# Output projection: two reloads of input rows moved ahead of the loads of a stored operand

## The chip, the cores and the metric

The kernel runs on one core of a Trainium2 chip. A core has a matrix engine (TensorE, PE in the profile), three engines for elementwise work (VectorE or DVE, ScalarE or ACT, GpSimd or POOL), SyncE (SP), which here only issues DMA transfers, and 16 DMA engines that move data between DRAM and the on-chip memory. Each engine works through its own instructions in a fixed order and waits on semaphores for the others. The metric is the time on the device in microseconds (us); the median of several runs is compared.

## The reference

One layer of a hybrid encoder, in float32, on 1024 tokens with 1024 channels. The part that matters here is the output projection and what follows it:

```python
merged = g_a * (o_sb @ w_o_sb) + g_b * (o_hg @ w_o_hg)
h = x + merged @ w_out
hn = rmsnorm(h, norm2_g)
a = square(relu(hn @ w_ff1))
h = h + a @ w_ff2
```

All matrices of `h = x + merged @ w_out` are 1024 x 1024.

## The kernel before

**Arithmetic.** Each float32 operand is split into a high part (a cast on ACT, line 144) and a low part (a subtraction on DVE, line 149). A product is three matmuls per tile: high by high, high by low, low by high (`three`, line 510). The helper `sub` or `add` shows in the profile as line 1118 or 1115, every matmul as line 121, and every load on SP's queue as line 129.

**The output projection** (`out_start`, line 1559) is computed by a scheme of seven half-size products: `merged` and `w_out` are cut in four quarters, sums of quarters are formed beforehand, and each product has 512 x 512 x 512 elements. It is done in four row blocks of 128 tokens (`tb` 0 to 3); a product of one block is 12 matmuls (`out_product`, line 1541). The blocks run through these passes:

1. `oW` (pwW in the profile): product "11" by "11", into one PSUM bank for each block. ACT copies the bank twice to `hres[tb]`, and DVE subtracts it from `hres[4 + tb]`, which holds the x rows of this block (line 1577).
2. `oW` again: "12" by "21" is added into the same bank. PE may start a block of it only after DVE's subtraction of pass 1 has read the bank.
3. `oX` (pwX): "2" by "2" into a new bank, followed by a subtraction on DVE.
4. `oX` again: "3" by "3" on top, with a subtraction, then "a" by "4".
5. `oY` (pwY): "1" by "1", then "4" by "22" (`out_block_done`, line 1623). Each finished block is squared and summed on ACT, its inverse root is taken on POOL, and DVE normalises it (`norm2_token`, line 1485). PE then transposes the normalised rows (`hnt`).

**Where the operands come from.** The x rows are reloaded from DRAM into the tiles `h4` to `h7` (`hres[4]` to `hres[7]`, in the order of the row blocks 1 to 4). The operands "2", "3", "a", "1" and "4" of `merged` (`m2r`, `m3r` and so on) are sums of quarters that the stage before formed. POOL stored them to DRAM (`fd`, `put`, line 1438), and SP loads them back (`out_operands`, line 1518). The last of these stores is issued at the end of the gate stage, so the second load of each operand has to wait for it. The weights "2", "3", "4", "1" (`wout2r` and so on) come from DRAM as well (`tw`).

**What sets the order.** `load` (line 128) chains every load on SP behind the load before it, so SP issues them in the order of the program text. A load that waits for a store holds all loads behind it. `in_turn` (line 135) fixes the order on ACT and DVE in the same manner. For row block 2, `out_operands(m=["2"], behind=True)` (line 1581) issues the two loads of "2" at once and leaves its splits for after the loop. In the loop of pass 1 the loads stand so on SP: h4, two of wout21, two of wout2, h5, two of m2, h6, h7, then two of wout3 and two of m3. POOL adds x rows to `hres[0]` to `hres[3]` with accumulating transfers (line 1596), which run at the same time.

Of the kernel before, what the change touches and what calls it, by code (L numbers as in the profile page):

```python
# [22 lines left out]
NT = T // P  # L23
# [16 lines left out]
def kernel(  # L40
# [20 lines left out]
    X = x[0]  # L61
# [13 lines left out]
    def slot(name, dt=F32):  # L75
        return spool.tile([P, 1024], dt, tag="s", name=name)
# [7 lines left out]
    def bank(name):  # L84
        return psum.tile([P, 512], F32, tag="p", name=name)
# [12 lines left out]
    def after(ins, earlier):  # L98
        if earlier is not None and earlier.ins is not ins.ins:
            tc.add_manual_dep(ins.ins, earlier.ins.name, NOSYNC, reason="issue order")  # L100
        return ins
# [26 lines left out]
    def load(dst, src):  # L128
        last_load[0] = after(nc.sync.dma_start(dst, src), last_load[0])
# [5 lines left out]
    def in_turn(engine, ins):  # L135
        if turns["on"]:
            after(ins, turns[engine])
            turns[engine] = ins
        return ins
# [12 lines left out]
    def hi_lo(h, l, src):  # L152
        hi_copy(h, src)
        return lo_sub(l, src, h)
# [300 lines left out]
    class Stream:  # L455
# [6 lines left out]
        def add(self, units, body):  # L462
            self.jobs.append((units, body))
            return len(self.jobs)
# [652 lines left out]
    def sub(out, a, b):  # L1117
        return nc.vector.tensor_tensor(out=out, in0=a, in1=b, op=ALU.subtract)
# [15 lines left out]
    def out_block(i, j):  # L1134
        return W_OUT[i * 512 : (i + 1) * 512, j * 512 : (j + 1) * 512]
# [342 lines left out]
    hres = []  # L1478
# [32 lines left out]
    def out_unit(name, src):  # L1511
        pieces = [src[i * 256 : (i + 1) * 256, :].rearrange("(k p) c -> p k c", p=P) for i in range(2)]
        return Unit(f"wout{name}", [[(0, 512, t)] for t in pieces], wide=True)
# [4 lines left out]
    def out_operands(w=(), m=(), behind=False):  # L1518

        for n in w:  # L1520
            out_form[n] = out_unit(n, tw[int(n)] if len(n) == 1 else out_block(int(n[0]) - 1, int(n[1]) - 1))
            out_form[n].split()
        for n in m:
            merged[n] = []
            raw = []
            for kp in range(2):
                r = slot(f"m{n}r{kp}")
                load(r.rearrange("p (k t) -> p k t", k=2), fd[n][kp])
                h, l = slot(f"m{n}h{kp}", F32R), slot(f"m{n}l{kp}", F32R)
                merged[n].append((h, l))  # L1530
                raw.append(r)

            def split(n=n, raw=raw):
                for (h, l), r in zip(merged[n], raw):
                    hi_lo(h, l, r)

            if behind:
                return split
            split()

    def out_product(ps, a, w, tb, start):
        open_block("fill")
        for k in range(4):
            c = k % 2 * 512
            sh, sl = (t[:, c + tb * P : c + (tb + 1) * P] for t in merged[a][k // 2])
            wh, wl = (t[:, c : c + 512] for t in out_form[w].hl[k // 2])
            three(ps, sh, sl, wh, wl, start and k == 0, k == 3, True)


    def rows(tb):  # L1550
        return slice((tb + 4) % NT * P, ((tb + 4) % NT + 1) * P)
# [4 lines left out]
    def turn_dve(ins):  # L1556
        in_turn("dve", ins)

    def out_start():

        merged["11"] = [mgs.t[0, kp] for kp in range(2)]
        merged["12"] = [mgs.t[0, kp] for kp in range(2, 4)]
        for tb in range(NT):
            hres.append(slot(f"h{tb}"))
        for tb in range(4):
            load(hres[4 + tb], X[rows(4 + tb), :])
            if tb == 0:
                out_operands(["21"])
            oW[tb] = bank(f"pwW{tb}")
            out_product(oW[tb], "11", "11", tb, True)  # L1570
            for ins in (
                nc.scalar.activation(hres[tb][:, right], oW[tb], AF.Identity, scale=-1.0),
                nc.scalar.copy(hres[tb][:, left], oW[tb]),
            ):
                in_turn("act", ins)
            h = hres[4 + tb][:, right]
            turn_dve(sub(h, h, oW[tb]))
            if tb == 0:
                out_operands(["2"])
            if tb == 1:  # L1580
                m2 = out_operands(m=["2"], behind=True)
        m2()
        for tb in range(4):
            out_product(oW[tb], "12", "21", tb, False)
            h = hres[4 + tb][:, left]
            turn_dve(add(h, h, oW[tb]))
            if tb == 0:
                out_operands(["3"])
            if tb == 1:
                out_operands(m=["3"])  # L1590
        for tb in range(4):
            oX[tb] = bank(f"pwX{tb}")
            out_product(oX[tb], "2", "2", tb, True)
            h = hres[4 + tb][:, right]
            turn_dve(sub(h, h, oX[tb]))
            nc.gpsimd.dma_start(hres[tb], X[rows(tb), :], accum_op=ALU.add)
            if tb == 0:
                out_operands(["4"])
            if tb == 1:
                out_operands(m=["a"])  # L1600
        for tb in range(4):
            out_product(oX[tb], "3", "3", tb, False)
            h = hres[tb][:, right]
            turn_dve(sub(h, h, oX[tb]))
            if tb == 0:
                out_operands(["1"])
            if tb == 1:
                out_operands(m=["1"])
            if tb > 1:
                pairs[tb - 2].load()  # L1610

        for tb in range(4):
            u = pairs[tb % 2]
            (u.split if tb < 2 else u.sums)()
            out_product(oX[tb], "a", "4", tb, False)
            h = hres[tb][:, left]
            turn_dve(add(h, h, oX[tb]))
            if tb == 2:
                out_operands(["22"])
            if tb == 3:  # L1620
                out_operands(m=["4"])
# [489 lines left out]
    first = pairs[:2]  # L2111
    turns["on"], turns["act"], turns["dve"] = True, None, None
    out_start()
    g2b[0] = slot("g2b")
    load(g2b[0], norm2_g[0].partition_broadcast(P))
# [91 lines left out]
```

## Time and profile before

The page gives the span of the profiled execution and no other time of it; the runs were timed apart.

| | |
|---|---|
| time, median of 3 runs | 1453.28 us (1452.68 to 1454.21) |
| span of the profiled execution | 1450.7 us |
| busy: PE, DVE, ACT, POOL | 1436.6, 1098.2, 669.8, 142.0 us |
| output projection, passes 1 to 4, on PE | from 742.9 to 803.9 us |
| DMA, mean over the span | 156 GB/s |

The span runs from the first to the last instruction of the program. Start times in the timeline are microseconds from its beginning; a row gives start, duration, engine, line, operation, tiles (written <- read), the form, the number of instructions merged in the row, and in brackets the engine's idle time before it with what ended it. "SPq" is SP issuing a transfer: the duration is that of the issue and not of the transfer, and where two issues are merged in one row, of all from the first to the last. The chain of waits follows the work that ended last from its end back to what released it. Rows of the windows view give, for a stretch of time, its length, the busy time of PE, of PE's weight loads, DVE, ACT and POOL, and at the end the granted clock of PE (1.00 is full), the busy share of the 16 DMA engines and their GB/s.

### The profile page before, as it was taken

The page shows a single profiled execution, that of the slowest core. Times are in us where ns is not written, and L with a number is a line of the kernel's source. Part 1 is how long each engine was busy: PE and PEld are TensorE (multiplying, and loading weights), DVE is VectorE, ACT ScalarE, POOL GpSimd, SP SyncE. Part 2 cuts the span into 40 slices and gives each one's busy share as a digit, 9 for nine tenths or more (in the row PEclk, how much of TensorE's full clock was granted, in tenths as well). Part 3 has the DMA queues.
Part 4 walks back from the last instruction along what each step waited for, and adds up shares of the span by engine and source line. Part 5 has one row for each costly group of instructions (what it writes and reads, how often), then busy time and mean ns, then how long its engine had stood idle before and what let it go on. Part 6 is the DMA issues. An engine that isn't in the chain of part 4 may idle for free.

```text
span 1450.7 us, 19961 instructions
## 1 busy us (share of the span) xinstructions
PE 1436.6 (99%) x7464; PEld 1222.6 (84%) x7464; DVE 1098.2 (76%) x1561; ACT 669.8 (46%) x1156; POOL 142.0 (10%) x340
## 2 busy tenths in 40 slices
PE   9999999999999999999999999999999999999998
PEld 8989988988898888888877888888888888888886
DVE  6699899798747797887757898666666757768765
ACT  7566666652323243533334575444444533523443
POOL 3121121110000012100010200000000000000032
PEclk9999999999999999999999999999999999999999
DMA  7234154321303349655479414344445974676825
GB/s 211 48 98 103 37 95 81 59 44 52 102 16 102 73 137 261 225 170 182 144 217 306 166 59 153 138 159 153 152 160 189 341 273 183 249 273 245 282 100 185
DMA packets 157881, 225.73 MB, mean 156 GB/s; under 512 B 25644, under 2 KB 93784, under 8 KB 157784
## 3 DMA queue, kind: packets, MB, share of 16 engines
q1 hardware_dynamic: 142520, 183.29, 37.3%
q0 software_dynamic: 11520, 34.61, 9.5%
q10 hardware_dynamic: 3744, 6.56, 1.2%
q8 instruction: 59, 0.97, 0.3%
q14 instruction: 38, 0.31, 0.1%
HBM read 162.55 MB, written 61.87 MB: 155 GB/s over the span
## 4 chain that ended last, share of the span: by engine, by line
PE 95%; DVE 1%; ACT 1%; DMA 1%; issue 1%; POOL 1%; POOLq 0%; DVEq 0%; ACTq 0%
PE pm L121 21%; PE pX L121 9%; PE pW L121 6%; PE pY L121 6%; PE pjqk L121 6%; PE pji L121 3%; PE pga L121 3%; PE pjq L121 3%; PE pys L121 3%; PE gY L121 3%; PE gX L121 3%; PE pyh L121 3%; PE pjf L121 3%; PE pjg L121 3%; PE sl L121 2%; PE po L121 2%
## 5 line engine op out<-in xcount | busy, mean ns | idle before, releaser
L144 ACT CAST whid<-w 128x1024 fp32r<-128x1024 f32 x30 | 31.6, 1053 | 153.0 <-PE pm L121 85.1
L709 DVE TENSOR_TENSOR_SCAN rm<-rm,bits 128x511 f32<-128x511 f32 (+7 forms) x72 | 87.3, 1220 | 14.3 <-ACT rm L687 12.8
L121 PE MATMUL pm<-wlod,sh 128*128 128x512 f32 x240 | 93.5, 390 | 0.0
L121 PE MATMUL pm<-whid,sl 128*128 128x512 f32 x240 | 93.4, 389 | 0.0
L121 PE MATMUL pm<-whid,sh 128*128 128x512 f32 x240 | 93.4, 389 | 0.0
L121 PE MATMUL pm<-th,sh 128*128 128x512 f32 x208 | 80.9, 389 | 0.0
L121 PE MATMUL pm<-tl,sh 128*128 128x512 f32 x208 | 80.9, 389 | 0.0
L121 PE MATMUL pm<-th,sl 128*128 128x512 f32 x208 | 80.9, 389 | 0.0
L149 DVE TENSOR_TENSOR wlod<-w,whid 128x1024 fp32r<-128x1024 f32 x30 | 36.7, 1223 | 56.4 <-ACT whid L144 56.4
L149 DVE TENSOR_TENSOR sl<-sa,sh 128x1024 fp32r<-128x1024 f32 x56 | 68.3, 1220 | 0.8 <-ACT sh L144 0.8
L144 ACT CAST wTh<-pw 128x128 fp32r<-128x128 f32 (+3 forms) x96 | 44.4, 487 | 50.6 <-PE pw L124 43.0
L144 ACT CAST sh<-sa 128x1024 fp32r<-128x1024 f32 x56 | 57.2, 1046 | 7.8 <-DMA sa<-ad 7.8
L1868 POOL TENSOR_SCALAR fss<-fss 128x1 f32<-128x1 f32 x8 | 4.5, 561 | 562.4 <-ACT fsc L1863 561.8
L149 DVE TENSOR_TENSOR wTl<-pw,wTh 128x512 fp32r<-128x512 f32 (+3 forms) x96 | 50.8, 548 | 9.1 <-ACT wTh L144 6.4
L121 PEld LDWEIGHTS pm<-wlod,sh 128*128 128x128 f32 x240 | 45.0, 187 | 9.9 <-DVE wlod L149 0.4
L121 PEld LDWEIGHTS pm<-whid,sh 128*128 128x128 f32 x240 | 45.1, 188 | 9.4
L121 PEld LDWEIGHTS pm<-whid,sl 128*128 128x128 f32 x240 | 45.1, 188 | 9.3
L157 DVE TENSOR_TENSOR bt<-bt,rm 128x511 f32<-128x511 f32 (+7 forms) x72 | 48.9, 685 | 5.1 <-ACT bt L690 1.0
L121 PE MATMUL pX<-sql,t1h 128*128 128x512 f32 x128 | 50.0, 391 | 0.1
L121 PE MATMUL pX<-sqh,t1h 128*128 128x512 f32 x128 | 50.0, 390 | 0.0
L121 PE MATMUL pX<-sqh,t1l 128*128 128x512 f32 x128 | 49.8, 389 | 0.0
L687 ACT ACTIVATE rm<-z 128x511 f32<-128x511 f32 (+6 forms) x96 | 47.7, 502 | 4.6 <-DVE bt L157 2.0
(911 smaller groups left out, 4596.0 us busy)
## 6 DMA issues: line engine op xcount, KB each, us to landing
w<-in_w_ff_dram SPq DMA_DIRECT2D x72, 512.0 KB, 5.5
sa<-ad SPq DMA_DIRECT2D x56, 512.0 KB, 6.6
ad<-a SPq DMA_DIRECT2D x32, 256.0 KB, 2.0
ad<-s SPq DMA_DIRECT2D x16, 512.0 KB, 5.2
tw<-in_w_out_dram POOLq DMA_DIRECT2D x24, 256.0 KB, 3.8
x<-in_x_dram SPq DMA_DIRECT2D x8, 512.0 KB, 9.6
xnl<-xnh POOLq DMA_DIRECT2D x8, 512.0 KB, 9.8
pr<-pd SPq DMA_DIRECT2D x8, 512.0 KB, 5.9
```

The source lines that it names most:

```text
L121: return pe(nc.tensor.matmul(*a, **k))
L144: hi_last[0] = after(in_turn("act", nc.scalar.copy(dst, src)), hi_behind[0])
L149: nc.vector.tensor_tensor(out=dst, in0=src, in1=hi.bitcast(F32), op=ALU.subtract),
L157: return nc.vector.tensor_tensor(out=out, in0=a, in1=b, op=ALU.mult)
L687: nc.scalar.activation(rm[:, s0 + c0 - 1 : s0 + m - 1], z[:, c0:m], AF.Sigmoid, scale=-0.125)
L709: sc = nc.vector.tensor_tensor_scan(out=rr, data0=rr, data1=bits[:, 1024 - nk + a : 1024 - nk + b][:, ::-1], initial=rm[:, b : b + 1] if i ...
L1868: nc.gpsimd.tensor_scalar(out=ssq, in0=ssq, scalar1=1.0 / D, scalar2=EPS, op0=ALU.mult, op1=ALU.add)
```

## The change

The loads of h5, h6 and h7 are issued together in the second turn of the loop, where only h5 was issued before. The load of h4 stays in front.

```diff
         for tb in range(NT):
             hres.append(slot(f"h{tb}"))
+        load(hres[4], X[rows(4), :])
         for tb in range(4):
-            load(hres[4 + tb], X[rows(4 + tb), :])
             if tb == 0:
                 out_operands(["21"])
+            if tb == 1:
+                for t in range(5, NT):
+                    load(hres[t], X[rows(t), :])
             oW[tb] = bank(f"pwW{tb}")
             out_product(oW[tb], "11", "11", tb, True)
```

In the built program the order on SP is then h4, two of wout21, two of wout2, h5, h6, h7, two of m2, two of wout3, two of m3. The instructions of the other engines stand in the same order as before.

## The prediction

> **What bounds the kernel now.** I read the page first, then who waited for whom on TensorE (PE), then the chain of waits around that wait.
>
> ```profile
> span 1450.7 us, 19961 instructions
> PE 1436.6 (99%) x7464; PEld 1222.6 (84%) x7464; DVE 1098.2 (76%) x1561; ACT 669.8 (46%) x1156; POOL 142.0 (10%) x340
> ...
> PE pwW L121 <- DVE h L1118: 3.8, 1, 3.8
> PE warm L121 <- POOL ident masks.py:199: 2.2, 1, 2.2
> PE pjqk L121 <- DVE xnl L309: 0.5, 1, 0.5
> ```
>
> PE is busy for 99% of the span, so a change gains time only where PE stands still or runs slowly. The whole list of its waits has three rows; one, of 3.8 us, lies in the output projection, on the subtraction of line 1577 (the profile shows the helper's line, 1118). The timeline of PE shows what this wait leaves behind, and the windows give the clock.
>
> ```profile
> 758.82 0.39 PE L121 MATMUL pwW<-wout21h,msl 128*128 128x512 f32 x1
> 763.05 0.79 PE L121 MATMUL pwW<-wout21h,msh 128*128 128x512 f32 x1 [3.84 <-DVE h L1118]
> ...
> 767.48 0.63 PE L121 MATMUL pwW<-wout21l,msh 128*128 128x512 f32 x1
> 767.91 0.63 PE L121 MATMUL pwW<-wout21h,msl 128*128 128x512 f32 x1
> ...
> 771.32 0.39 PE L121 MATMUL pwX<-wout2h,m2h 128*128 128x512 f32 x1
> ...
> 771.48 32.64 PE pwX L121 x144
> ...
> 759.05:763.05 4.00, 0.16 (x2) 0.00 (x1) 0.69 (x1) 0.43 (x1) 0.00 (x0) 0.87 1.08 277
> 763.05:771.30 8.25, 8.25 (x24) 6.55 (x25) 5.19 (x6) 3.00 (x3) 0.00 (x0) 0.65 0.90 306
> ```
>
> In the window rows the last three numbers are granted clock, DMA share and GB/s. The 144 matmuls of the later row start 0.227 us apart, those behind the wait 0.43 us, at a mean granted clock of 0.65. So the wait costs twice: once as idle time, once as a slow stretch in which PE counts as fully busy.
>
> Why the subtraction was late stands in the DMA queue of SyncE (SP) and on VectorE (DVE).
>
> ```profile
> 740.01 0.42 SPq L129 DMA_DIRECT2D h<-in_x_dram  x1
> 740.52 10.12 SPq L129 DMA_DIRECT2D m2r<-fd  x2
> 750.73 1.06 SPq L129 DMA_DIRECT2D h<-in_x_dram  x2
> ...
> SPq L129 <- DMA fd<-yr: 9.3, 1, 9.3
> ...
> 749.98 0.68 DVE L1118 TENSOR_TENSOR h<-h,pwW 128x512 f32<-128x512 f32 x1
> 762.31 0.69 DVE L1118 TENSOR_TENSOR h<-h,pwW 128x512 f32<-128x512 f32 x1 [11.65 <-DMA h<-in_x_dram]
> 766.11 0.69 DVE L1118 TENSOR_TENSOR h<-h,pwW 128x512 f32<-128x512 f32 x1 [3.12 <-DMA h<-in_x_dram]
> 766.72 2.35 DVE L149 TENSOR_TENSOR m2l<-m2r,m2h 128x1024 fp32r<-128x1024 f32 x2
> ```
>
> The second load of operand "2" (m2r) holds SP for 9.3 us until GpSimd's (POOL's) store of that operand has landed. The two x loads behind it (h6, h7) go out at 750.73, and the DVE subtractions of row blocks 3 and 4 wait for them.
>
> **The change, part by part.** It removes and adds no instruction. PE, DVE, ACT and POOL issue the same operations in the same order in the built program. On SP alone, h6 and h7 move ahead of the two m2r loads; h5 stands where it stood. So three things must be priced: the earlier h6 and h7, the later m2r, and what is behind.
>
> *h6 and h7.* Their buffers are free: in the built program h6 waits for a matmul of the last gX group, h7 for nothing beyond that.
>
> ```profile
> 732.01 2.72 PE gX L121 x12
> ...
> DMA to landing us min/median/max: 3.0/3.9/11.2
> ```
>
> That group ends at 734.7, so both go out right behind h5, about 740.5 and 741.0 (SP spent 1.06 us on the two). The second row is the time to landing of the x loads of this stage. The shortest is 3.0 us, and even the longest, 11.2 us, gives 752.2. PE needs the third block's subtraction (0.69 us) at 759.05, so h6 may land as late as 758.3. **This wait goes whatever end of the range I take.**
>
> *What that is worth.* Idle time: the next matmul was due at 758.82 + 0.23 = 759.05 and started at 763.05, 4.00 us. Slow stretch: the 24 matmuls from 763.05 to 771.32 took 8.27 us; at the pace of the pwX row (32.64 / 144 = 0.2267 us) they take 5.44 us, so 2.83 us. Together **6.83 us**; the pwX products would start at 764.49.
>
> The Trainium skill, "TensorE: Matmul & The Clock Gate", Part 1, says that the clock falls to half after an idle window of about 3.4 us, that the window is free-running, and that it takes a busy window to rise. The 4.00 us of idle and the 0.65 above agree with it. By that rule a shorter new wait costs its own length only, and one past the window costs some 2.8 us more; rival D below works this out from the rows.
>
> *What is late next: the operand "2".* The first pwX product needs its second half (m2r, then a cast on ACT, then m2l) at its seventh matmul, 764.49 + 6 x 0.2267 = 765.85.
>
> ```profile
> 758.44 1.05 ACT L144 CAST m2h<-m2r 128x1024 fp32r<-128x1024 f32 x1 [2.55 <-DMA m2r<-fd]
> 767.73 1.05 ACT L144 CAST wout3h<-wout3r 128x1024 fp32r<-128x1024 f32 x1 [8.25 <-DMA wout3r<-tw]
> 769.08 1.05 ACT L144 CAST wout3h<-wout3r 128x1024 fp32r<-128x1024 f32 x1 [0.29 <-DMA wout3r<-tw]
> 770.41 2.25 ACT L144 CAST m3h<-m3r 128x1024 fp32r<-128x1024 f32 x2 [0.28 <-DMA m3r<-fd]
> ...
> fd<-yr POOLq DMA_DIRECT2D x3, 256.0 KB, 5.8
> ...
> 740.00:752.00 12.00, 12.00 (x54) 9.95 (x53) 9.13 (x13) 6.20 (x10) 4.50 (x7) 1.00 0.89 265
> 752.00:768.00 16.00, 12.16 (x44) 9.52 (x43) 2.58 (x4) 3.50 (x6) 1.74 (x2) 0.81 1.05 289
> ```
>
> Today it lands at 758.44; the cast (1.05) and m2l (1.2) make it ready at 760.7, 5.1 us early. The change puts 1 MB ahead of its DRAM store, whose landing (5.8 us from the issue) m2r waits for. Bounds: nothing, since 0.11 of the 12 us from 740 to 752 stands open (1.3 us) and m2r no longer shares with h6 and h7; or the full price of the two, each about 3.9 us apart when they landed in company (762.31 to 766.11 less the subtractions), 7.8 us. I take 1.5 us, nearer the open end, as the loads go out 0.5 to 3.5 us ahead of m2r's store, into the only stretch with open DMA time: with 5.1 us to spare, cost nothing. At 7.8 us PE would stall 2.7 us.
>
> The Trainium skill, "DMA: Bandwidth & Descriptors", Queues, rings and completion order, says that each DMA engine takes turns between the queues that have work. That speaks against the change: a longer SP queue halves the stores' share at 746 to 750. An estimate by that page: while both queues have work, the stores get half, and the delay is about 2 us; the sum would be the same.
>
> *Behind it: wout3 and m3.* Their loads no longer have h6 and h7 in front. The two places behind m2r landed at 762.3 and 766.1 (h6, h7: the ends of the two DVE waits); wout3r can now take them, and its two casts began at 767.73 and 769.08. The second one gains 3.0 us, which I take; the bounds are nothing (the DMA share is 1.05 from 752 to 768, so the same work may end no sooner) and 4.3 us (the open 1.3 us on top). They feed a longer chain: wout3's split frees the buffers of wout4r, which lands and is split ahead of the subtractions that PE waits for in the second pwX pass.
>
> ```profile
> 780.88 0.68 DVE L1118 TENSOR_TENSOR h<-h,pwX 128x512 f32<-128x512 f32 x1
> 784.03 1.88 DVE L1118 TENSOR_TENSOR h<-h,pwX 128x512 f32<-128x512 f32 x3
> ...
> 784.92 0.39 PE L121 MATMUL pwX<-wout3h,m3h 128*128 128x512 f32 x1
> ...
> 787.64 0.39 PE L121 MATMUL pwX<-wout3h,m3h 128*128 128x512 f32 x1
> ...
> 790.04 0.62 ACT L144 CAST b11h<-w_0r 128x512 fp32r<-128x512 f32 x1 [0.46 <-DMA w_0r<-in_w_ff_dram]
> ...
> 793.28 0.69 DVE L1118 TENSOR_TENSOR h<-h,pwX 128x512 f32<-128x512 f32 x1 [1.64 <-PE pwX L121]
> 793.89 0.69 DVE L149 TENSOR_TENSOR b11l<-w_0r,b11h 128x512 fp32r<-128x512 f32 x1
> ...
> 814.38 1.29 DVE L1503 SCALAR_TENSOR_TENSOR hn<-h,n_y,g2b 128x1024 f32<-128x1024 f32 x1
> ...
> 817.57 0.60 PE L124 MATMUL hnt<-ident,hn 128*128 128x128 f32 x4
> ```
>
> Blocks 2 and 3 of that pass start at 784.92 and 787.64; their subtractions end at 781.56 and about 784.65. The slack is 3.4 and 3.0 us, so if PE comes 6.8 us earlier this chain must come 3.8 us earlier. With 3.0 us it falls short by 0.8 us, with 4.3 us by nothing: I take the middle, **0.4 us** of new wait; bounds 0 and 3.8 us (no shift at all). The last five rows are the next narrow place: the second normalised block ends at 815.67, 1.9 us before its transposes, so it has to come 4.9 us earlier. In DVE's fixed order its work follows the subtraction at 793.28, which waits for PE and moves with it; the row after that needs a cast that ended at 790.66, 3.2 us before, so 3.2 us are there even if its load comes no sooner, and 1.7 us would be missing; with the load 1.7 us earlier, nothing. I take nothing, and the missing 1.7 us lies inside the bound above, since a wait there would overlap and not add. PE's list has no wait behind this stage, so a shift made here is kept to the end.
>
> **The sum.** 4.00 + 2.83 - 0.40 = 6.4 us off the profiled span of 1450.7 us, 1444.3 us. The median of the runs, 1453.28, stands 2.6 us above that span (start and end around it, untouched): **1446.9 us**.
>
> **The rivals.**
> *B, the bound moves to the second pwX pass.* The DMA engines have a fixed amount to move (share over 1 from 752 to 768), so wout3, wout4 and the operand "a" come hardly earlier, and PE waits 2 to 3.8 us for the subtractions there. For it: the two slacks above. Against it: wout3r takes the queue place of h6 and h7. Gain 3.0 to 4.8 us: about 1449.3.
> *C, slower.* m2r waits for POOL's store; with 1 MB in front of that store, the operand comes after PE needs it and the clock falls again. Beyond a delay of 5.1 us PE stalls, beyond 5.1 + 3 (the window row of the wait shows the clock lowered for the last 1.04 of its 4.00 us, 0.13 x 4.00 / 0.5) the slow stretch of 2.83 us is paid as well, and from 9.1 us (stall 4.0 + 2.83) the gain is eaten. At 10 us it ends at 1454.2. Against it: twice 3.9 us is only 7.8.
> *D, the same.* Rival B's wait reaches 3 us or more in one piece, so the clock halves there: 6.83 - 3.4 - 2.83 = 0.6 us gain, 1452.7. Against it: two subtractions share the wait, so that it comes in two pieces.
> *E, the change doesn't do what it says*: h6 and h7 still land late, as their buffers or queue are taken, 1453.3. The gX row speaks against it.
>
> **How the numbers follow.** Forecast 0.68, B 0.18, C 0.04, D 0.05, E 0.05. The forecast alone spans 1446.2 to 1448.2 (all of 6.83 to 5 us); to leave out no more than 2 in 10 the range takes in most of B: 1446.0 to 1450.0. About 0.2% (2.9 us, what a measurement of this kernel can tell from no change) is passed by the forecast and by B, 0.86; D, E and a rest of C are the same, 0.10; slower 0.04.
>
> **What would show it.** Right: the two x loads issue near 741 in SP's timeline, no PE wait on pwW, granted clock 1.00 from 759 to 771, the first pwX matmul near 764.5. Operand "2" later by 0 to 3 us, wout3's casts near 765. Wrong: a PE wait on pwX after an m2l (C), or on pwX after a DVE subtraction near 778 to 782 (B, and D if the clock drops behind it).

## The result, and the profile after

The changed kernel takes 1449.16 us (median of 9 runs, 1447.22 to 1450.87), the kernel before 1453.15 us (9 runs, 1451.76 to 1454.21). The ratio is 0.9973, with a 95% interval of 0.9964 to 0.9981. So 4.0 us are gained, between 2.8 and 5.2 by the interval. The forecast was 6.4 us.

First the head of the page of after, then the list of PE's waits (us in total, times, longest), whole but for two rows.

```profile
span 1447.2 us, 19961 instructions
```

```profile
PE gX L121 <- DVE gu L1115: 1.0, 1, 1.0
PE pwX L121 <- DVE h L1118: 0.8, 1, 0.8
PE pjqk L121 <- DVE xnl L309: 0.8, 1, 0.8
PE pX L121 <- DVE sql L149: 0.3, 1, 0.3
PE hnt L124 <- DVE hn L1503: 0.2, 1, 0.2
```

The wait of 3.8 us on pwW is gone. In its place stand small waits on pwX, hnt and pX, all on DVE and all behind the place of the change. One on gX, in the gate stage, stands ahead of it.

The SP timeline of after shows the new order of the loads, and the windows show the stretch in which the clock had been low.

```profile
741.40 1.37 SPq L129 DMA_DIRECT2D h<-in_x_dram  x3
742.88 11.37 SPq L129 DMA_DIRECT2D m2r<-fd  x2
754.35 1.05 SPq L129 DMA_DIRECT2D wout3r<-tw  x2
```

```profile
740.00:752.00 12.00, 12.00 (x54) 9.94 (x54) 10.47 (x14) 5.29 (x8) 4.34 (x7) 1.00 0.91 315
752.00:768.00 16.00, 16.00 (x72) 13.23 (x72) 4.47 (x6) 4.59 (x7) 1.90 (x3) 1.00 1.05 282
```

h5, h6 and h7 go out together at 741.40. From 740 to 768 PE is busy throughout at a granted clock of 1.00, where the second window had stood at 0.81 before. The DMA share is 0.91 and 1.05, hardly other than before (0.89 and 1.05).

PE's timeline of after has the first pwX matmul and the two new waits:

```profile
765.88 0.39 PE L121 MATMUL pwX<-wout2h,m2h 128*128 128x512 f32 x1
...
779.25 0.39 PE L121 MATMUL pwX<-wout3h,m3l 128*128 128x512 f32 x1
780.46 0.50 PE L121 MATMUL pwX<-wout3h,m3h 128*128 128x512 f32 x1 [0.82 <-DVE h L1118]
...
813.39 0.27 PE L124 MATMUL hnt<-ident,hn 128*128 128x128 f32 x1
813.89 1.86 PE L124 MATMUL hnt<-ident,hn 128*128 128x128 f32 x15 [0.23 <-DVE hn L1503]
```

To compare profiles, the table gives the time from one stage's first matmul to the next one's, read from PE's timeline of every profile: pwW, pwX, pwY, pW (first product of the MLP) and pX (the next). "All" is from pwW to pX, "start" is where pwW begins. The rows below "after" are experiments, told in the next section.

| profile | start | pwW to pwX | pwX to pwY | pwY to pW | pW to pX | all |
|---|---|---|---|---|---|---|
| before | 742.73 | 28.59 | 32.64 | 25.30 | 17.28 | 103.80 |
| before, again (b_again) | 744.17 | 29.14 | 32.64 | 25.30 | 17.28 | 104.35 |
| after | 744.12 | 21.76 | 33.91 | 25.76 | 17.35 | 98.78 |
| after, again (a_again) | 743.00 | 21.76 | 33.13 | 26.92 | 17.37 | 99.17 |
| e_h6 | 743.91 | 26.35 | 32.65 | 25.30 | 17.28 | 101.58 |
| e_fill | 743.13 | 27.15 | 32.64 | 25.30 | 17.28 | 102.37 |
| e_early | 743.11 | 21.76 | 32.71 | 26.48 | 17.36 | 98.32 |
| e_early once more (e_early_sums) | 743.90 | 21.76 | 32.64 | 25.30 | 17.28 | 96.98 |
| e_sums | 742.79 | 21.76 | 34.31 | 25.30 | 18.09 | 99.44 |
| e_roomy | 742.80 | 21.76 | 33.64 | 25.29 | 17.28 | 97.97 |
| e_best | 742.90 | 21.76 | 32.64 | 25.30 | 18.09 | 97.78 |
| e_early_roomy | 742.81 | 21.76 | 32.64 | 25.29 | 17.28 | 96.97 |
| e_early_roomy_yr | 742.94 | 21.76 | 32.64 | 25.29 | 17.28 | 96.97 |

The column pwW to pwX falls by 6.83 us, to the hundredth what was forecast. The next three give 1.27 + 0.46 + 0.07 = 1.80 us back in after and 0.49 + 1.62 + 0.09 = 2.20 us in its second profile. From pX to the product behind it both lose another 0.35 us (6.10 us before, 6.45 in both). So about **2.2 to 2.6 of the 6.8 us are given back** within about 105 us, where 0.4 was forecast. The span shows only 3.5 us, mostly because pwW starts 1.39 us later in this profile than in that of before; b_again, below, shows that this is chance.

### The profile page after: what moved, and what is told of

Same layout as the page of the kernel before. It is cut to its first block, busy times and chain, and to the rows that moved or that the text cites. A ratio compares the mean times of both kernels' runs of the same rounds, so it can differ in the third digit from the quotient of the medians.

```text
span 1447.2 us, 19961 instructions
## 1 busy us (share of the span) xinstructions
PE 1434.0 (99%) x7464; PEld 1219.8 (84%) x7464; DVE 1098.0 (76%) x1561; ACT 669.7 (46%) x1156; POOL 142.3 (10%) x340
```

## The experiments

**Theory:** the change takes away all of the 6.83 us, and what is given back comes from loads that are late in turn. wout4, which takes the buffers that wout3 leaves, is late for the subtractions in pwX, and wout1, which takes those of wout4, is late for DVE's row of work that leads to the normalised blocks (hnt). **Rivals:** the slow clock was worth something else than 2.83 us; or the new waits are chance that no load sets; or DVE's own row is too long whatever the loads do.

### Both kernels again

a_again is the changed kernel, with more runs; b_again is the kernel before, one run with its profile.

> The changed kernel once more, unaltered. In its first profile PE reached the first pwW matmul at 744.12 us, against 742.73 before, after a 1.0 us wait on gX at 733, which lies ahead of everything that the change moves. Theory: that wait is chance (a POOL store that lands sooner or later), so it comes and goes from one execution to the next, and the stretch from the first pwW to the first pwX matmul stays at 21.8 us against 28.6 before. Rival: the change causes the wait; then pwW starts near 744.1 again. Ratio to the kernel before 0.9965 to 0.998 by both.

> The kernel before once more, for a second profile. Theory: the wait of 3.8 us on pwW and the slow stretch behind it are there again, 28.6 us from pwW to pwX give or take 1 us, and nothing waits behind it, since the late start of pwX covers the two later loads; pwW may start anywhere from 742.7 to 744.2, as the wait on gX near 733 comes and goes with the landing of a POOL store. Rival (the slow stretch depends on where the wait falls against a clock window): 25.7 us in a profile with the clock at 1.00.

a_again: 1449.04 us (6 runs) against 1453.31 (22 runs), ratio 0.9973 (0.9961 to 0.9984). Of its PE timeline, the wait at hnt:

```profile
811.49 0.27 PE L124 MATMUL hnt<-ident,hn 128*128 128x128 f32 x1
813.15 1.86 PE L124 MATMUL hnt<-ident,hn 128*128 128x128 f32 x15 [1.39 <-DVE hn L1503]
```

The 6.83 us come back exactly. What is given back is of the same size and lies elsewhere: little in pwX, more at hnt.

b_again took 1455.07 us (one run). The waits of PE in b_again:

```profile
PE pwW L121 <- DVE h L1118: 4.5, 1, 4.5
...
PE gX L121 <- DVE gu L1115: 0.8, 1, 0.8
```

Here the kernel before has the gX wait, which its first profile didn't have, and starts pwW at 744.17, as late as after did. The instructions up to this place stand in the same order in both kernels. So the 1.39 us that hide a part of the gain in the first pair of spans are **chance from run to run, and no effect of the change**. In the pair a_again and b_again the spans differ by 6.8 us instead (1446.5 and 1453.3), where chance goes the other way: there the kernel before starts pwW 1.17 us later than the changed one.

### e_h6: h7 left behind operand "2"

On the changed kernel, only h5 and h6 go ahead:

```diff
-                for t in range(5, NT):
+                for t in (5, 6):
                     load(hres[t], X[rows(t), :])
...
+            if tb == 3:
+                load(hres[7], X[rows(7), :])
```

> Only h6 goes ahead of the two m2 loads; h7 stays behind them. Theory (the waits overlap, and a short one costs only its length): h7 lands near 762 in the crowded stretch, PE waits 1 to 1.5 us for the fourth block of pwW, the clock stays at 1.00, pwW to pwX takes 22.5 to 23.5 us, and the later waits in pwX (1.3 us in the changed kernel) shrink by as much, so the whole is within 0.5 us of the changed kernel: ratio to the kernel before near 0.9975. Rival (waits add up): 1.3 us worse than the changed kernel, ratio near 0.998. Rival (any wait brings the half clock): 2.8 us worse on top, ratio near 1.0.

1450.9 us (11 runs), ratio 0.9981 (0.9972 to 0.999). PE's timeline of e_h6, then its windows:

```profile
762.73 0.39 PE L121 MATMUL pwW<-wout21h,msl 128*128 128x512 f32 x1
766.09 0.79 PE L121 MATMUL pwW<-wout21h,msh 128*128 128x512 f32 x1 [2.97 <-DVE h L1118]
```

```profile
762.00:765.50 3.50, 1.11 (x5) 0.57 (x4) 0.16 (x1) 0.50 (x1) 0.00 (x0) 1.00 1.05 256
765.50:769.00 3.50, 2.92 (x7) 2.34 (x8) 3.42 (x5) 1.05 (x1) 0.00 (x0) 0.51 1.04 404
769.00:773.00 4.00, 4.00 (x20) 3.25 (x19) 3.87 (x4) 3.16 (x3) 0.00 (x0) 1.00 0.68 234
```

A short wait at full clock was expected; that was a miss. h7 alone, issued at 753.16 on SP, landed no sooner for being alone: DVE's subtraction of the fourth block, which waits for it, starts at 765.34, 12.2 us later, where h6 took 11.6 us with h7 beside it in before (750.73 to 762.31). PE waited 2.97 us and the clock fell. So h7 has a wait of its own, which in before lay hidden under that of h6 and the slow stretch behind it. **It is not enough that h6 goes ahead: h7 alone in the old place costs most of the gain** (4.59 of 6.83 us here). h6 alone in the old place was not run. The stages behind are clean again, as PE comes to them later.

### e_fill: the clock kept up in the kernel before

On the kernel before, PE runs 14 extra matmuls into an empty bank while it would wait; nothing reads their result.

```diff
+            if tb == 2:
+                open_block("fill")
+                spare = bank("spare")
+                for _ in range(14):
+                    matmul(
+                        spare, merged["12"][0][0][:, 0:P], out_form["21"].hl[0][0][:, 0:512],
+                        start=True, stop=True,
+                    )
```

> The kernel before, with 14 extra matmuls into a bank that nobody reads, put ahead of the third block of the second pwW pass, where PE waited 4.0 us (they take 14 x 0.227 = 3.2 us; their results are not used). The loads stand as before. Theory: the wait for h6 stays, but PE is busy in it, the clock stays at 1.00, and the slow stretch of 2.83 us goes: pwW to pwX 25.5 to 26 us against 28.6, ratio to the kernel before near 0.998. Rival (the slow stretch has another cause than the idle time): no gain, ratio 1.000, clock below 1 behind the wait. Rival (the gain is given back later all the same): pwX comes 2.8 us earlier, but the end moves by less than 2 us.

1451.67 us (11 runs), ratio 0.9992 (0.9983 to 1.0), which the times alone hardly tell from no gain; the profile tells more. PE's timeline of e_fill and its windows:

```profile
759.45 3.33 PE L121 MATMUL spare<-wout21h,msh 128*128 128x512 f32 x14
763.60 0.50 PE L121 MATMUL pwW<-wout21h,msh 128*128 128x512 f32 x1 [0.81 <-DVE h L1118]
...
767.41 0.50 PE L121 MATMUL pwW<-wout21h,msh 128*128 128x512 f32 x1 [0.79 <-DVE h L1118]
```

```profile
760.00:764.00 4.00, 3.19 (x15) 2.33 (x14) 0.69 (x1) 0.00 (x0) 0.00 (x0) 1.00 1.06 279
764.00:768.00 4.00, 3.21 (x15) 2.32 (x14) 1.33 (x2) 0.22 (x1) 0.00 (x0) 1.00 1.04 358
```

The clock stays at 1.00, and pwW to pwX falls from 28.59 to 27.15 us, by 1.44 instead of 2.83. The rest turns into the second wait, at 767.41, for h7. The slow stretch of before was real, but about half of it covered that wait. Idle time and slow stretch together were worth 6.83 us only because the change moved both loads.

### e_early: the same loads in the idle DMA stretch before

On the changed kernel the three loads move one turn up, ahead of wout2:

```diff
             if tb == 0:
                 out_operands(["21"])
-            if tb == 1:
                 for t in range(5, NT):
                     load(hres[t], X[rows(t), :])
```

> As changed, but h5, h6 and h7 also go ahead of the two wout2 loads: they are issued near 732 to 735, when the DMA engines stand nearly idle, and not at 741, ahead of POOL's stores. Theory (the 2 us that the changed kernel loses again in pwX and behind it come from DMA work that piles up from 744 to 768): m2r lands 2 us or more sooner than 761.9, wout3r's casts start before 766 (767.6 in the changed kernel), the wait on pwX near 780 goes or is under 0.3 us, pwX takes 32.7 to 33.0 us instead of 33.9, and the whole is 1 to 2 us better than the changed kernel: ratio to the kernel before near 0.9962. Rival (that wait is set by DVE's order, in which the subtraction stands behind the split of wout4): pwX stays at 33.5 us or more and the whole within 0.5 us of the changed kernel.

1447.56 us (5 runs), ratio 0.996 (0.9947 to 0.9972). The window of before shows the room that is used, those of e_early show it filled (the last two numbers are the DMA share and GB/s):

```profile
736.00:740.00 4.00, 4.00 (x19) 3.31 (x18) 4.00 (x6) 1.77 (x3) 0.00 (x0) 1.00 0.36 119
```

```profile
736.00:740.00 4.00, 4.00 (x20) 3.30 (x19) 4.00 (x6) 2.16 (x3) 0.00 (x0) 1.00 1.03 402
740.00:752.00 12.00, 12.00 (x55) 9.93 (x54) 9.51 (x13) 5.82 (x10) 4.52 (x7) 1.00 0.80 241
```

ACT's casts in e_early and in after show what came earlier:

```profile
759.11 1.05 ACT L144 CAST m2h<-m2r 128x1024 fp32r<-128x1024 f32 x1 [2.83 <-DMA m2r<-fd]
...
767.23 1.05 ACT L144 CAST wout3h<-wout3r 128x1024 fp32r<-128x1024 f32 x1 [0.96 <-DMA wout3r<-tw]
...
775.29 1.05 ACT L144 CAST wout4h<-wout4r 128x1024 fp32r<-128x1024 f32 x1 [3.04 <-DMA wout4r<-tw]
```

```profile
761.92 1.05 ACT L144 CAST m2h<-m2r 128x1024 fp32r<-128x1024 f32 x1 [4.64 <-DMA m2r<-fd]
767.55 1.05 ACT L144 CAST wout3h<-wout3r 128x1024 fp32r<-128x1024 f32 x1 [4.58 <-DMA wout3r<-tw]
768.76 1.05 ACT L144 CAST wout3h<-wout3r 128x1024 fp32r<-128x1024 f32 x1 [0.17 <-DMA wout3r<-tw]
...
777.50 1.05 ACT L144 CAST wout4h<-wout4r 128x1024 fp32r<-128x1024 f32 x1 [2.31 <-DMA wout4r<-tw]
...
785.77 1.05 ACT L144 CAST wout1h<-wout1r 128x1024 fp32r<-128x1024 f32 x1 [2.89 <-DMA wout1r<-tw]
```

pwX to pwY is 32.71 us, almost its length without a wait, against 33.1 to 34.3 in the four profiles with the loads in the place of after. So the wait in pwX hangs on **where the three x loads are issued**. DVE in after shows what PE waits for:

```profile
778.58 1.23 DVE L149 TENSOR_TENSOR wout4l<-wout4r,wout4h 128x1024 fp32r<-128x1024 f32 x1 [1.71 <-ACT wout4h L144]
779.73 0.68 DVE L1118 TENSOR_TENSOR h<-h,pwX 128x512 f32<-128x512 f32 x1
```

The subtraction whose end lets PE go on at 780.46 stands behind the split of wout4's second half, and this split waits for the cast that began at 777.50. From the start of pwW, that cast begins 33.38 us in after, 32.61 in a_again, 33.78 in e_sums, 33.11 in e_roomy and 32.18 in e_early. What lies above 32.11 us is, in all five, what pwX takes over 32.64 us, within 0.01 us. So **the second half of wout4 sets the size of this wait**. wout3, whose buffers wout4 takes, doesn't set it alone: its second cast comes later in a_again than in after (25.20 and 24.64 us), and the wait there is shorter. In the five profiles with the loads of e_early wout4's cast comes at 30.2 to 32.2 us, in the four with those of after at 32.6 to 33.8. That it comes sooner because the DMA engines are less full from 740 to 768 is argued, not shown: their share from 740 to 752 is 0.80 here and 0.91 in after, but 0.94 in the second profile of e_early, and from 752 to 768 it is 1.03 here and 1.05 in after.

The wait at hnt stays in this profile (0.94 us).

What ran under the label e_early_sums was this same kernel once more, so that only its profile tells something:

> The kernel of e_early once more, for a second profile of it: pwW to pwX 21.8 us, pwX 32.7 us, no wait on pwX over 0.3 us, and a wait on hnt of about 1 us, since DVE's row of work is as long as before. Rival (the clean pwX of the first profile was chance): pwX 33.1 us or more, as in the two profiles of the changed kernel.

1447.41 us (one run). pwX is clean again (32.64), and this time hnt too. Without more room for wout1 the wait at hnt is a matter of the run: the second cast of wout1, which has to precede DVE's row towards hnt, began 41.2 us after the start of pwW in the one profile (784.28) and 38.5 us in the other (782.38).

### e_sums and e_roomy: two ways to an earlier hnt

e_sums shortens DVE's row ahead of the normalised blocks: on the changed kernel, sums of the MLP's weight parts move behind them.

```diff
-            (u.split if tb < 2 else u.sums)()
+            if tb < 2:
+                u.split()
...
+        if tb in (2, 3):
+            first[tb - 2].sums(turns["dve"])
```

> As changed, but the eight subtractions that form the sums of the first MLP weights (0.6 us each on DVE, 4.8 us) are moved behind the second normalised block. Theory (what the changed kernel loses behind pwX is DVE's unbroken row of work, about 22 us from the last split of wout1 to the second normalised block): that block comes 3 us or more earlier against the start of pwW, the wait on hnt (0.3 to 1.7 us from one profile to the next) goes, first pwY to first pW on PE takes 25.3 us as in the kernel before instead of 25.8 to 26.9; together with the wait on pwX that remains the whole gains 0.5 to 1.3 us over the changed kernel, ratio to the kernel before near 0.9965. Rival (the MLP's start needs these sums, DVE is full there too): what hnt gains, pX or pY loses again, 17.4 us from pW to pX grows to 18 or more, ratio 0.9973 or worse.

1447.84 us (7 runs) against 1452.79 (12 runs), ratio 0.9971 (0.996 to 0.9981). PE's timeline of e_sums:

```profile
826.43 1.86 PE L124 MATMUL hnt<-ident,hn 128*128 128x128 f32 x15 [0.58 <-DVE hn L1503]
```

The hnt wait at 813 is gone, but the moved work comes back as one at 826.43, and pW to pX grows by 0.81 us. The work moved behind on the same engine is only paid later here; no gain over the changed kernel from pwW to pX (99.44 against 98.78 and 99.17), and the ratio to the kernel before is the same as well.

e_roomy leaves DVE's row as it is and lets wout1 be loaded into a larger set of buffers, so that its second load no longer waits for the splits of wout4:

```diff
         for n in w:
...
+            if n == "1":
+                out_form[n].roomy = (0, 1)
             out_form[n].split()
```

> As changed, but the two loads of wout1 go into buffers of the large pool instead of the pair of load buffers, so that they don't wait until wout4 is split. Rival theory (the late normalised block comes from the wait for wout1's landing, after which DVE's row starts): wout1's second cast begins 2 us or more before 785, DVE's gap of 1.3 to 2.2 us ahead of its split goes, hnt waits less by as much. If DVE's row alone sets it: the same as the changed kernel within 0.5 us, as the row is as long as before and is filled from other loads. If the large pool has no buffer free: wout1 comes later and the whole is 1 to 4 us slower than the changed kernel. Ratio to the kernel before 0.9965 if the rival holds, 0.9973 if not.

1446.38 us (6 runs), ratio 0.9963 (0.995 to 0.9976). DVE in after, and in e_roomy:

```profile
786.85 1.22 DVE L149 TENSOR_TENSOR wout1l<-wout1r,wout1h 128x1024 fp32r<-128x1024 f32 x1 [1.25 <-ACT wout1h L144]
...
812.55 1.28 DVE L1503 SCALAR_TENSOR_TENSOR hn<-h,n_y,g2b 128x1024 f32<-128x1024 f32 x1
```

```profile
782.80 2.35 DVE L149 TENSOR_TENSOR wout1l<-wout1r,wout1h 128x1024 fp32r<-128x1024 f32 x2
...
809.62 1.28 DVE L1503 SCALAR_TENSOR_TENSOR hn<-h,n_y,g2b 128x1024 f32<-128x1024 f32 x1
```

From the end of wout1's split to the second normalised block it is 812.55 - 788.07 = 24.48 us in after and 809.62 - 785.15 = 24.47 us in e_roomy. DVE's row has the same length; it starts earlier, since both halves of wout1 are there. In all seven profiles in which the three loads go ahead and this row is left as it is, the stretch is 24.46 to 24.49 us, so the second hn moves with the end of wout1's split and with nothing else. The two casts of wout1 begin 1.35 or 1.36 us apart in the three profiles with this edit, and 2.55 to 4.62 us apart in the six of the changed order without it, so that its second half being there in time is not chance. The hnt wait is gone (25.29 us). That speaks against the rival that the row is too long in itself, and shows **wout1's second load as what sets the hnt wait**. The wait in pwX stays (33.64), as this edit doesn't touch wout3 or wout4.

### Both parts together

e_early_roomy has the edits of e_early and e_roomy. e_best has those of e_early and e_sums, and e_early_roomy_yr those of e_early_roomy, both with one more: the loads of wout11 go ahead of the last load that waits for a store in the gate stage, to take away the chance wait on gX.

```diff
             for t, d in ((self.p, pd), (self.y, yd)):
+                if self is gates_in[-1] and d is yd:
+                    out_form["11"].load()
                 load(t.rearrange("p (k t) -> p k t", k=2), d[cb])
```

> Three things together: h5 to h7 ahead of the two wout2 loads as in e_early, the eight subtractions behind the second normalised block as in e_sums, and the two wout11 loads ahead of the last load that waits for a POOL store in the gate stage (the wait of PE on gX near 733, 0 to 1.0 us, is laid to that load). Theory: the gains add, since each takes away another wait: no PE wait on gX, pwW, pwX or hnt over 0.3 us, 6.8 us less than the kernel before up to hnt and kept from there: ratio 0.9950 to 0.9955 (1446 us or just below). Rival: DVE is full at the start of the MLP and takes 1 us or more back; ratio near 0.996, that of e_early.

> h5 to h7 ahead of the two wout2 loads (as in e_early) and wout1 loaded into the large pool (as in e_roomy). Theory (after the changed kernel two loads are late in turn: wout3 behind the crowded stretch, which holds the subtractions of pwX, and wout1 behind its buffers, which holds the first normalised pair): both waits go, from the first pwW to the first pX matmul PE takes 97.0 us, against 103.8 in the kernel before and 98.7 to 99.2 in the two profiles of the changed kernel; 6.8 us less than the kernel before, ratio 0.9953. Rival (something else still comes late, DVE's row for one): 98 us or more, ratio 0.996 as for e_early and e_roomy alone.

> The same, and the two wout11 loads ahead of the last gate load that waits for a POOL store. Theory: as e_early_roomy, and PE never waits on gX near 733 (0, 0.5, 0.7 or 1.0 us and 0.4 us on top in the profiles so far); pwW starts at 742.7 to 743.2. On average 0.3 to 0.6 us better than e_early_roomy, within its interval. Rival: the wait on gX comes back although wout11 is early, if it is not wout11 that it hangs on.

e_best: 1446.81 us (5 runs), 0.9964 (0.9952 to 0.9977). e_early_roomy: 1446.26 us (5 runs) against 1452.68 (9 runs), 0.9957 (0.9945 to 0.997). e_early_roomy_yr: 1446.16 us (5 runs, 1445.56 to 1446.47), 0.9955 (0.9941 to 0.9968). The whole list of PE's waits in e_early_roomy:

```profile
PE warm L121 <- POOL ident masks.py:199: 2.2, 1, 2.2
PE pjqk L121 <- DVE xnl L309: 1.0, 1, 1.0
```

From pwW to pX it takes 96.97 us, 6.83 less than before: with both loads mended, **all that the change took away is kept** in this stretch. e_best still pays e_sums' wait (18.09). The gX wait is in neither of the two profiles with the last edit, but e_early_roomy's profile hasn't got it either, so that the edit's own worth is not settled. The last two versions can't be told apart. Their medians are the lowest, though the interval of e_roomy (1446.38 us) overlaps theirs; from pwW to pX they are 1.8 us shorter than after and 2.2 us shorter than a_again.

## Why the prediction was right, and where it was wrong

1. *h6 and h7 land in time, 6.83 us.* Right in every profile of the changed order: pwW to pwX is 21.76 us, which is 96 matmuls at the full pace of 0.2267 us. The parts 4.00 and 2.83 don't stand for themselves, though: e_fill and e_h6 show that h7's own wait lay under the slow stretch.
2. *Operand "2" 1.5 us later, at no cost.* Right in effect, small in size. From the start of pwW its second cast comes 15.7 and 16.4 us behind in the two profiles of before (758.44, 760.56), and 17.8 and 18.1 in the two of after (761.92, 761.06): about 1.9 us later, within the 5.1 to spare. The estimate of 2 us worked out from the Trainium skill, "DMA: Bandwidth & Descriptors", Queues, rings and completion order, agrees with that in size, though no run shows the turns between the queues themselves; e_early, with those loads out of the way, brings it back to 16.0 us.
3. *wout3's chain 3.0 us earlier.* Too much. Its second cast comes 26.4 and 25.9 us behind the start of pwW before (769.08, 770.02), and 24.6 and 25.2 after (768.76, 768.20): 1.2 us earlier. The places on SP's queue moved up, but the engines behind it were full until 768 (share 1.05, as before), which was the lower bound's reason. The new wait in pwX is 1.27 and 0.49 us, 1.7 and 1.0 in e_sums and e_roomy, where 0.4 was taken. The wait follows wout4's second cast, as e_early shows, and there the 3.8 us that the prediction asked of this chain are right (35.93 us after the start of pwW in before, 32.11 without a wait); the cast came 2.55 us earlier in after and 3.32 in a_again. What was mis-sized is how much earlier the chain comes, which the prediction read off wout3 alone.
4. *The second normalised block: "I take nothing".* **This step failed.** The prediction had the numbers: the block must come 4.9 us earlier, 3.2 are there, 1.7 are missing. It then put the 1.7 us at nothing, by an earlier load and by an overlap with the wait in pwX. Overlap was right, but a wait of 0.4 us covers 0.4 of 1.7. From the start of pwW the second hn begins at 71.65 us in before (814.38), and at 68.43 in after, 68.81 in a_again and 67.96 in e_early. That is 3.22, 2.84 and 3.69 us earlier, so 1.7, 2.1 and 1.2 short of 4.9. That the 3.22 us of after meet the 3.2 of the prediction is luck. The prediction took its 3.2 from a cast of w_0r, for which DVE waits in none of these profiles; in after the 3.22 are 1.49 us by which wout1's split ends earlier (45.44 and 43.95 us from the start of pwW) and 1.73 us by which the row behind it is shorter (26.21 and 24.48), since DVE no longer waits 1.64 us for PE in it. The waits in pwX and at hnt together are 1.73, 2.11 and 1.25. The shift of this one block sets the sum of both, and how it is split between the two places is chance. Where the block comes in time, the wait in pwX alone is paid (1.00 us in e_roomy).
5. *"PE's list has no wait behind this stage, so a shift is kept to the end."* Not quite: pX, about 30 us later, loses another 0.4 us, again on DVE. Work that isn't late at the old pace can be at the new one. With wout1 in time (e_roomy, e_early_roomy) this wait goes too.

With 1.7 to 2.1 in place of 0.4, and the 0.4 at pX, the sum would have been 6.83 - 2.2 to 2.6, a gain of 4.2 to 4.6 us; the medians say 4.0 (2.8 to 5.2) and 4.3. The measured 1449.16 us lies outside the 1446.2 to 1448.2 that the forecast alone spanned; it lies in the stated range only through the room left there for rival B. It is nearly the time of rival B (1449.3), but its mechanism is only half of it: the wait in pwX is 0.5 to 1.7 us where B had 2 to 3.8, and the rest is paid at a place that the forecast counted as free. C and D did not come about; E is ruled out by the SP timeline.

Two small readings of the prediction are off, and neither moves the forecast much. The 2.6 us between span and median are not all start and end: time and span of one and the same run differ by 1.7 to 1.9 us in every run on record, and the rest is a profiled run that was quicker than the median. And the two x loads landed 3.8 us apart (762.31 to 766.11), not 3.9.

## What to carry to other kernels

When a stall is removed, list every later place with less slack than the gain, and charge the largest shortfall among them, not the first: waits in a row overlap, and the largest one sets the sum. A load that moves up in a queue need not gain what the places are worth (1.2 us instead of 3.0 here, with the DMA share at 1.05); look for a stretch where that share is low, as the 0.36 here, and try it there. Where the gain was given back by a late operand, more room for its load mended it here, while moving other work behind on the same engine did not.

## What the hardware showed that was not expected

The clock did not fall after the same length of waiting each time. In before it fell at 762.0, 2.9 us after the next matmul was due. In e_h6 a pause of 3.13 us between matmuls (762.96, where the next was due, to 766.09) was enough, and the clock was down already at 765.5, 2.5 us into it. The Trainium skill, "TensorE: Matmul & The Clock Gate", Part 1, asks for an idle window of about 3.4 us; no such window fits into this pause, so here the measurement decides, and a wait of 3 us is to be priced as one that may cost the clock. The stretch at half clock had two lengths: 3.4 us in e_h6 (765.5 to 768.9), and twice that in before (762.0 to 768.8) and, after 4.5 us of waiting, in b_again, as its windows show:

```profile
759.00:763.80 4.80, 1.65 (x8) 1.03 (x6) 0.00 (x0) 1.04 (x1) 0.00 (x0) 1.00 1.04 272
763.80:770.63 6.83, 5.46 (x13) 4.30 (x14) 3.77 (x5) 1.66 (x2) 0.00 (x0) 0.50 1.03 355
```

The pause of about a microsecond in pwX left the clock of after at 1.00 and cost a little more than its length: the matmul that resumes at 780.46 takes 0.50 us instead of 0.39, and the next one, at 780.80, starts 0.34 us behind it instead of 0.23.
